# Causal masks of the state-space decays: from mask products on TensorE to ScalarE copies into a PSUM bank of their own

## The chip, the cores and the metric

The kernel runs on one core of one Trainium2 chip. Its engines work side by side and wait for each other by semaphores: TensorE (PE; its weight loads are shown as PEld), VectorE (DVE), ScalarE (ACT), GpSimd (POOL) and SyncE (SP), which issues the DMAs. The metric is the device time of one execution in microseconds (us), here the median of several runs.

## The reference

Two transformer blocks run one after the other on 256 tokens of width 1024. The first has a mixer of sparse and latent attention, cross attention to a memory, and hierarchical experts. The second block joins the result with 256 context tokens and runs two layers: a Mamba-2 state-space mixer (SSD) over both samples and in both directions, then attention; each followed by an expert layer. The change lies in the SSD, whose core in the reference is this:

```python
a = jnp.moveaxis(dtc * A.reshape(SSD_GROUPS, SSD_HPG), 2, -1)
acum = jnp.cumsum(a, axis=-1)
tri = jnp.tril(jnp.ones((Q, Q), dtype=bool))
seg = jnp.exp(jnp.where(tri, acum[..., :, None] - acum[..., None, :], -jnp.inf))
cb = jnp.einsum('bclgn,bcsgn->bcgls', Cc, Bc)
y_diag = jnp.einsum('bcgrls,bcsgrp->bclgrp', cb[:, :, :, None] * seg, xdt)
```

There are 8 groups of 4 heads, chunks of 128 tokens, a state of 128. The projection ahead of it is 1024 x 6208, with a convolution of width 5 over time and silu; behind it come a gate with silu(z), an RMS norm and an output projection of 2048 x 1024. `seg` is the causal mask and the decay in one: positions after the row's own get exp of minus infinity, which is 0.

## The kernel before, in words

The second block's first layer is the SSD. Features lie on partitions and the 512 tokens (256 context, 256 of the sample) along the free axis. Products whose inputs are float32 are done as three products of split halves (`mm3`, L1301 to L1303), so a projection piece of 128 features is 24 products of 512 columns.

`ssd` first normalises and transposes, then calls `ssd_steps` (L1343), which computes the step sizes dt of all heads (L1301 to L1303 into tile `wdt`), their exp and log chain (L1372 to L1385 on ScalarE and VectorE), the transposes of dt (L1390), the running sums by triangular products (L1401) and, for each of the two directions, the factors of the exponents: `RR` (the rows), `LB` and `FL` (the columns), and the state's coefficients, transposed on TensorE at L1445. Then the eight groups follow. `ssd_project` computes six pieces of 128 features for a group (weight split by ScalarE L1295 and VectorE L1296, convolution, tanh), and `ssd_group` its scan. For a chunk's half and each of its two key blocks `ssd_group` forms three exponents, each as one product of `LBg` and `RR` (L1562): two diagonal ones, forward and backward, and one off the diagonal. On a diagonal exponent the mask (bfloat16, 0 or a large negative number) is added by a second product with the identity into the same bank (L1565). ScalarE takes the Exp (L1567), GpSimd adds both diagonals (L1569), VectorE multiplies with B times C (L1572, tile `M`), and TensorE multiplies M with x into the output (L1575). After the groups `ssd_out` (L1616) projects back.

All order on the engines is set by a scheduler that simulates the program's time line and moves instructions within what their tiles allow; it is not written by hand. So instructions of `ssd_steps`, of group 0's projection, and of neighbouring groups lie mixed in the engines' queues. What limits it are the pools: memory tiles and the eight PSUM banks. All of this layer uses one PSUM pool `four`, with two banks for each of the tags p (projections), y (outputs of a group), b (exponents and small products) and t (transposes and products of the states).

The lines that the change and the prediction touch are L1526 to L1613 in `ssd_group`, L1312 in `ssd`, and the pool in `run`.

Of the kernel before, what the change touches and what calls it, by code (L numbers as in the profile page):

```python
# [22 lines left out]
AF = mybir.ActivationFunctionType  # L23
# [7 lines left out]
T = 256  # L31
# [47 lines left out]
class Net:  # L79
# [1229 lines left out]
    def pool(self, name, side=None):  # L1309
        return self.tc.tile_pool(name=name, bufs=1, side=side, reuse_waits="tile")  # L1310

    def ssd(self, right):  # L1312
        nc, a = self.nc, self.a
        self.piece = -1
        with self.pool("ssdh") as hp, self.pool("ssdx") as xp, self.pool("ssd") as pool, ExitStack() as q:
            tile_, x_ = self.cut(pool), self.cut(xp)
            pp = q.enter_context(self.pool("ssdq", "right"))
            self.ada_tile, self.ada_ps = lambda: self._t(pp, [P, 2 * D], "adaw", 1), "p"
            hT = [self.cut(hp)([P, 8, 512], f"hT{v}", 1, F32R) for v in range(2)]
            for r, xx in ((1, self.ctx_x), (0, self.x)):  # L1320
                rows = self.norm_halves([xx[:, 0], xx[:, 1]], lambda: x_([P, 512], "xbc", 8), self.ctx_r if r else None)
                m, sh = self.mod_cols(0, 0, r)
                self.to_features_mod(rows, m, sh, hT, (1 - r) * T, lambda: x_([P, 512], "z", 4)[:, :T])
            with self.pool("ssdr") as rp:
                self.load_const("const_b", rp)
                tmp_ = self.cut(rp)
                A4 = self.arena(rp, 3)
                self.ada_step(1)
                self.ssd_steps(tile_, tmp_, A4, hT)
            with self.pool("ssdg") as gp:  # L1330
                self.yd = [self.dp.tile([P, 2, 512], F32, name=f"yd{g}") for g in range(7)]
                self.sqa = self.cut(gp)([P, 512], "sqa")
                nc.gpsimd.memset(self.sqa, 0.0)
                for g in range(8):
                    parts = self.ssd_project(g, self.cut(pp), self.cut(xp), hT)
                    if g == 7:
                        q.close()
                        op = right.enter_context(self.pool("ssdo", "right"))
                        self.y7 = self.cut(op)([P, 2, 512], "y7")
                    self.ssd_group(g, *parts, self.cut(gp), self.cut(op) if g == 7 else None)  # L1340
        return self.cut(op), op

    def ssd_steps(self, tile_, tmp_, A4, hT):  # L1343
# [180 lines left out]
    def ssd_group(self, g, xs, BT, CT, zz, tile_, last=None):  # L1524
        nc = self.nc
        dsk, nw = self.colv("ssd_D_2"), self.colv("ssd_norm_w_2")  # L1526
        xtm = tile_([P, 2, 4, P], "xtm", 1)
        for c in range(2):
            p = self.ps("t").rearrange("p (i f) -> p i f", i=4)
            for i in range(4):  # L1530
                nc.tensor.transpose(p[:, i], xs[c][:, i * P:(i + 1) * P], self.ident)
            nc.scalar.activation(xtm[:, c], p, AF.Copy)
        btm = tile_([P, 2, P], "btm", 2)
        p = self.ps("t")[:, :T].rearrange("p (i f) -> p i f", i=2)
        for i in range(2):
            nc.tensor.transpose(p[:, i], BT[:, i * P:(i + 1) * P], self.ident)
        nc.vector.tensor_copy(btm, p)
# [1 line left out]
        for d in range(2):  # L1539
            t = tile_([P, 768], "LBg", 2, F32R)  # L1540
            nc.vector.tensor_scalar(t, self.LB[d], self.grp[:, g:g + 1], None, op0=OP.mult)
            LBg.append(t)
            t = tile_([P, 256], "FLg", 2, F32R)
# [3 lines left out]
        for q in range(2):  # L1547
            p = self.ps("b").rearrange("p (s l) -> p s l", s=2)
            for st in range(2):
                i = 2 * q + st  # L1550
                nc.tensor.matmul(p[:, st], lhsT=BT[:, i * P:(i + 1) * P], rhs=CT[:, q * T:(q + 1) * T],
                                 start=True, stop=True)
            cb = tile_([P, 2, T], "cb", 2)
            nc.scalar.activation(cb, p, AF.Copy, scale=0.25)
            for st in range(2):
                M = tile_([P, 4, T], "M", 2)
                ex = []

                for d, var, lt, diag in ((0, 2 * q + st, st, True), (1, 2 * q + st, st, True),
                                         (st, 4 + q, 1 - st, False)):  # L1560
                    p = self.ps("b").rearrange("p (r l) -> p r l", r=4)
                    nc.tensor.matmul(p, lhsT=LBg[d][:, var * P:(var + 1) * P], rhs=self.RR[d][:, :, 2 * q + lt],  # L1562
                                     start=True, stop=not diag)
                    if diag:
                        nc.tensor.matmul(p, lhsT=self.identb, rhs=self.maskb[:, d], start=False, stop=True)  # L1565
                    e = tile_([P, 4, P], "seg", 3)
                    nc.scalar.activation(e, p, AF.Exp)  # L1567
                    ex.append((e, lt))
                nc.gpsimd.tensor_tensor(ex[0][0], ex[0][0], ex[1][0], op=OP.add)  # L1569
                for e, lt in (ex[0], ex[2]):  # L1570
                    s = slice(lt * P, (lt + 1) * P)
                    nc.vector.tensor_tensor(M[:, :, s], e, cb[:, st, None, s].to_broadcast([P, 4, P]), op=OP.mult)  # L1572
                for c in range(2):
                    for par in range(2):
                        nc.tensor.matmul(yps[c][par * 64:par * 64 + 64, q * T:(q + 1) * T],  # L1575
                                         lhsT=xtm[:, c, 2 * q + st, par * 64:par * 64 + 64], rhs=M[:, 2 * c + par],
                                         start=(st == 0), stop=(st == 1))

        hs = tile_([P, 2, 256], "hs", 1)
        for d in range(2):  # L1580
            p = self.ps("b")[:, :256]
            for i in range(2):
# [5 lines left out]
                                 start=(i == 0), stop=(i == 1))  # L1588
            nc.scalar.activation(hs[:, d], p, AF.Copy)
        for c in range(2):  # L1590
# [2 lines left out]
                nc.tensor.matmul(p[:, d], lhsT=self.pairs[:, c], rhs=FLg[d], start=True, stop=True)  # L1593
            eF = tile_([P, 2, 256], "eF", 2)
            nc.scalar.activation(eF, p, AF.Exp)
            p = self.ps("t").rearrange("p (d l) -> p d l", d=2)
            for d in range(2):
                nc.tensor.matmul(p[:, d], lhsT=hs[:, d, c * P:(c + 1) * P], rhs=CT[:, T:], start=True, stop=True)
            nc.vector.tensor_tensor(eF, eF, p, op=OP.mult)
            y, ch = xs[c], 2 * g + c  # L1600
# [471 lines left out]
    def run(self):  # L2072
# [2 lines left out]
        self.small = "b"  # L2075
        nc = self.nc
        four = dict(p=2, y=2, b=2, t=2)
        with ExitStack() as right, self.psum(**four):
            out_, _ = self.ssd(right)
            ap = self.ctx.enter_context(self.pool("attt"))  # L2080
            with self.pool("ch0") as pool, self.weight_slots(2), ExitStack() as more:
                o = self.choice(0, [(self.ctx_x, 1), (self.x, 0)], pool)
                with self.pool("chs0") as tp:
                    tmp_ = self.cut(tp)
                    self.ssd_out(0, out_)
                    self.choice_route(o, 0, tmp_)
                    self.ssd_out(1, out_)
                    self.attention_tables(ap)
                    right.close()
                    more.enter_context(self.weight_slots(4, "right"))  # L2090
                    self.choice_route(o, 1, tmp_)
                more.enter_context(self.weight_slots(1, "right"))
                self.hold = [self.ctx_x[:, 1, 1023:]] * 2
                with self.pool("chf0") as fp:
                    self.choice_run(o, self.cut(fp))
                self.hold = None
# [56 lines left out]
```

## Time and profile before

| | us |
|---|---|
| median of 3 runs | 2184.37 (2181.54 to 2187.75) |
| the profiled execution | 2188.18 |
| its span | 2186.4 |
| PE busy | 1886.7 (86%) |
| DVE busy | 967.2 (44%) |
| ACT busy | 634.0 (29%) |
| POOL busy | 456.7 (21%) |

The span is the time from the first to the last instruction in the trace; the execution's own time holds 1.8 us more around it. The share of busy time is an average over stages: up to about 1010 us the engines share the work of mixers and the SSD, from 1100 to 1500 and from 1760 to 2100 the expert layers stream weights at 426 GB/s and the DMA engines are busy all the time. The SSD's steps lie at about 464 to 519 us, its groups at 516 to 922, its output projection from 922 on. A matmul's duration in the rows holds its way through the array; in a dense stream the distance between two starts tells what one costs.

### The profile page before, as it was taken

Reading aid. Unit: us, or ns where it says so; the run is one execution under the profiler, and the core shown is the slowest. Engines: PE = TensorE matmul, PEld = TensorE weight load, DVE = VectorE, ACT = ScalarE, POOL = GpSimd, SP = SyncE. Lnnn points to the kernel's source line nnn. Section 1 sums busy time; section 2 is a strip of 40 time slices with the busy share of each in tenths; the row PEclk is TensorE's granted clock in tenths of the full one; section 3 lists DMA queues with packets and bytes.
Section 4 is the critical chain, followed back from the end, with each engine's and each line's share of the span. In section 5 each row is a group of like instructions: output and inputs, shape, how many; then the busy total and the mean of one; then the engine's idle time right before and its main releaser. Section 6 shows DMA issues by size and latency. Waiting matters only on the chain. (4 is left out here: it accounts for less than half of the span.)

```text
span 2186.4 us, 23839 instructions
## 1 busy us (share of the span) xinstructions
PE 1886.7 (86%) x9107; PEld 1033.4 (47%) x9128; DVE 967.2 (44%) x1643; ACT 634.0 (29%) x1174; POOL 456.7 (21%) x483
## 2 busy tenths in 40 slices
PE   7989879989999999889799898997989767667666
PEld 6767644356667777567333333333755411111111
DVE  6776642169777787566322222222676301010101
ACT  6545422154544455444100000001454200000000
POOL 4341020023232333422111111101653100000000
PEclk9999989999999999999899999999899889899989
DMA  7554748853232321275799999997537799999996
GB/s 243 179 191 148 294 171 327 365 166 97 87 107 62 127 92 54 88 237 199 317 428 426 426 427 426 428 427 308 223 126 288 288 428 426 429 427 428 427 425 278
DMA packets 131078, 603.49 MB, mean 276 GB/s; under 512 B 18563, under 2 KB 59222, under 8 KB 92558
## 3 DMA queue, kind: packets, MB, share of 16 engines
q1 hardware_dynamic: 130958, 601.91, 69.7%
q8 instruction: 73, 1.20, 0.2%
q14 instruction: 47, 0.39, 0.0%
HBM read 597.09 MB, written 4.78 MB: 275 GB/s over the span
## 5 line engine op out<-in xcount | busy, mean ns | idle before, releaser
L1818 PE MATMUL ps<-w,xg 128*64 128x512 f32 (+1 forms) x2048 | 452.8, 638 | 111.0 <-DMA w<-in_moe_w_dram 111.0
L1818 PEld LDWEIGHTS ps<-w,xg 128*64 128x64 f32 (+1 forms) x2048 | 130.6, 127 | 394.2 <-issue 236.0
L1871 POOL TENSOR_TENSOR x<-x,o 128x512 f32<-128x512 f32 x24 | 38.9, 1621 | 651.4 <-DVE o L1870 651.4
L1301 PE MATMUL ps<-hT,ws 128*128 128x512 f32 x384 | 157.8, 411 | 3.5 <-DVE ada L1236 3.2
L1302 PE MATMUL ps<-hT,ws 128*128 128x512 f32 x384 | 157.8, 411 | 0.0
L1303 PE MATMUL ps<-hT,ws 128*128 128x512 f32 x384 | 155.9, 406 | 0.0
L1818 PE MATMUL ps<-w,ctx 128*32 128x512 f32 x512 | 107.0, 656 | 36.9 <-DMA w<-in_moe_w_dram 35.9
L1818 PE MATMUL ps<-w,actT 128*64 128x512 f32 x512 | 124.4, 596 | 4.0 <-DMA w<-in_moe_w_dram 2.1
L1861 DVE SCALAR_TENSOR_TENSOR y<-ps,s,y 128x512 fp32r<-128x512 f32 x24 | 17.9, 748 | 247.6 <-ACT y L1860 247.6
L1507 DVE SCALAR_TENSOR_TENSOR conv<-pad,cols,conv 128x512 f32<-128x512 f32 x124 | 111.9, 903 | 2.6 <-ACT conv L1500 0.4
L1860 ACT ACTIVATE y<-ps,s 128x512 fp32r<-128x512 f32 x24 | 16.5, 686 | 322.8 <-PE ps L1818 246.6
L1301 PEld LDWEIGHTS ps<-hT,ws 128*128 128x128 f32 x384 | 73.1, 190 | 25.7 <-issue 4.0
L1870 DVE TENSOR_TENSOR o<-ps,g 128x512 f32<-128x512 f32 x80 | 52.3, 686 | 69.2 <-PE ps L1867 66.2
L1302 PEld LDWEIGHTS ps<-hT,ws 128*128 128x128 f32 x384 | 73.4, 191 | 19.1 <-issue 3.8
L1296 DVE TENSOR_TENSOR ws<-wr,ws 128x1024 fp32r<-128x1024 f32 x48 | 62.3, 1299 | 44.5 <-ACT ws L1295 37.9
L1303 PEld LDWEIGHTS ps<-hT,ws 128*128 128x128 f32 x384 | 73.2, 191 | 18.2 <-issue 1.9
L1818 PEld LDWEIGHTS ps<-w,ctx 128*32 128x32 f32 x512 | 25.2, 115 | 113.4 <-DMA w<-in_moe_w_dram 58.2
L1818 PEld LDWEIGHTS ps<-w,actT 128*64 128x64 f32 x512 | 43.0, 136 | 74.9 <-issue 66.5
L1569 POOL TENSOR_TENSOR seg<-seg,seg 128x512 f32<-128x512 f32 x32 | 47.1, 1471 | 116.5 <-ACT seg L1567 101.7
L1296 DVE TENSOR_TENSOR ws<-w,ws 128x1024 fp32r<-128x1024 f32 x46 | 61.5, 1342 | 22.0 <-ACT ws L1295 21.4
L1567 ACT ACTIVATE seg<-ps 128x512 f32<-128x512 f32 x96 | 54.8, 597 | 51.3 <-PE ps L1562 16.1
L1850 DVE TENSOR_TENSOR ctx<-ctx,ps 128x512 f32<-128x512 f32 x8 | 5.5, 686 | 141.9 <-PE ps L1818 141.9
(639 smaller groups left out, 3712.7 us busy)
## 6 DMA issues: line engine op xcount, KB each, us to landing
w<-in_moe_w_dram SPq DMA_DIRECT2D x164, 2048.0 KB
w<-in_moe_w_dram SPq DMA_DIRECT2D x56, 1024.0 KB
v<-in_ada_w_dram SPq DMA_DIRECT2D x32, 512.0 KB
w<-in_moe_w_up_dram SPq DMA_DIRECT2D x16, 1024.0 KB
w<-in_moe_w_gate_dram SPq DMA_DIRECT2D x16, 1024.0 KB
w<-in_moe_w_down_dram SPq DMA_DIRECT2D x16, 1024.0 KB
wr<-in_ssd_in_w_dram SPq DMA_DIRECT2D x16, 1024.0 KB
w<-in_ssd_out_w_dram SPq DMA_DIRECT2D x32, 512.0 KB
```

The lines of the kernel that those rows point to most:

```text
L1296: (eng or self.nc.vector).tensor_tensor(lo, x, hi.bitcast(F32), op=OP.subtract)
L1301: t.matmul(p, lhsT=L[0], rhs=R[0], start=start, stop=False, **kw)
L1302: t.matmul(p, lhsT=L[0], rhs=R[1], start=False, stop=False, **kw)
L1303: t.matmul(p, lhsT=L[1], rhs=R[0], start=False, stop=stop, **kw)
L1507: nc.vector.scalar_tensor_tensor(seq(cv), pad[:, :, j:j + 256], tap(j), seq(cv), op0=OP.mult, op1=OP.add)
L1567: nc.scalar.activation(e, p, AF.Exp)
L1569: nc.gpsimd.tensor_tensor(ex[0][0], ex[0][0], ex[1][0], op=OP.add)
L1818: nc.tensor.matmul(p[j * S:(j + 1) * S], lhsT=x(k, j), rhs=ws[j // ne][:, j % ne, k % nk, n * 512:(n + 1) * 512], start=(k == 0), stop=(k ...
L1860: nc.scalar.activation(y[:, 0], p, AF.Copy, scale=ws)
L1861: nc.vector.scalar_tensor_tensor(y[:, 1], p, ws, y[:, 0].bitcast(F32), op0=OP.mult, op1=OP.subtract)
L1870: nc.vector.tensor_tensor(o, q, gr[s][:, c], op=OP.mult)
L1871: (nc.gpsimd if i else nc.vector).tensor_tensor(xx[:, i, c], xx[:, i, c], o, op=OP.add)
```

## The change

For the groups alone the PSUM pools are closed and others opened: p and y keep two banks, b has three, and one bank, m, is allotted once as `self.seg` for all diagonal exponents. The tag t is gone in the groups; what used it takes b. After the groups the old four tags are opened again. On a diagonal exponent ScalarE copies the mask into the bank first (L1571 of the new kernel), and the exponents' product (L1572) is added onto it with `start=False`; the mask's own product is gone. The first diagonal of all still has a mask product, once (L1569), so that the bank is marked as written. The Exp (L1575) reads the bank as before.

```diff
@@ -1309,7 +1309,7 @@
     def pool(self, name, side=None):
         return self.tc.tile_pool(name=name, bufs=1, side=side, reuse_waits="tile")
 
-    def ssd(self, right):
+    def ssd(self, right, banks):
         nc, a = self.nc, self.a
         self.piece = -1
         with self.pool("ssdh") as hp, self.pool("ssdx") as xp, self.pool("ssd") as pool, ExitStack() as q:
@@ -1327,6 +1327,10 @@
                 A4 = self.arena(rp, 3)
                 self.ada_step(1)
                 self.ssd_steps(tile_, tmp_, A4, hT)
+            banks.close()
+            banks.enter_context(self.psum(p=2, y=2, b=3, m=1))
+
+            self.seg = self.ps("m").rearrange("p (r l) -> p r l", r=4)
             with self.pool("ssdg") as gp:
                 self.yd = [self.dp.tile([P, 2, 512], F32, name=f"yd{g}") for g in range(7)]
                 self.sqa = self.cut(gp)([P, 512], "sqa")
@@ -1338,6 +1342,8 @@
                         op = right.enter_context(self.pool("ssdo", "right"))
                         self.y7 = self.cut(op)([P, 2, 512], "y7")
                     self.ssd_group(g, *parts, self.cut(gp), self.cut(op) if g == 7 else None)
+            banks.close()
+            banks.enter_context(self.psum(p=2, y=2, b=2, t=2))
         return self.cut(op), op
 
     def ssd_steps(self, tile_, tmp_, A4, hT):
@@ -1526,12 +1532,12 @@
         dsk, nw = self.colv("ssd_D_2"), self.colv("ssd_norm_w_2")
         xtm = tile_([P, 2, 4, P], "xtm", 1)
         for c in range(2):
-            p = self.ps("t").rearrange("p (i f) -> p i f", i=4)
+            p = self.ps("b").rearrange("p (i f) -> p i f", i=4)
             for i in range(4):
                 nc.tensor.transpose(p[:, i], xs[c][:, i * P:(i + 1) * P], self.ident)
             nc.scalar.activation(xtm[:, c], p, AF.Copy)
         btm = tile_([P, 2, P], "btm", 2)
-        p = self.ps("t")[:, :T].rearrange("p (i f) -> p i f", i=2)
+        p = self.ps("b")[:, :T].rearrange("p (i f) -> p i f", i=2)
         for i in range(2):
             nc.tensor.transpose(p[:, i], BT[:, i * P:(i + 1) * P], self.ident)
         nc.vector.tensor_copy(btm, p)
@@ -1558,11 +1564,13 @@
 
                 for d, var, lt, diag in ((0, 2 * q + st, st, True), (1, 2 * q + st, st, True),
                                          (st, 4 + q, 1 - st, False)):
-                    p = self.ps("b").rearrange("p (r l) -> p r l", r=4)
+                    p = self.seg if diag else self.ps("b").rearrange("p (r l) -> p r l", r=4)
+                    if diag and (g, q, st, d) == (0, 0, 0, 0):
+                        nc.tensor.matmul(p, lhsT=self.identb, rhs=self.maskb[:, d], start=True, stop=True)
+                    elif diag:
+                        nc.scalar.activation(p, self.maskb[:, d], AF.Copy)
                     nc.tensor.matmul(p, lhsT=LBg[d][:, var * P:(var + 1) * P], rhs=self.RR[d][:, :, 2 * q + lt],
-                                     start=True, stop=not diag)
-                    if diag:
-                        nc.tensor.matmul(p, lhsT=self.identb, rhs=self.maskb[:, d], start=False, stop=True)
+                                     start=not diag, stop=True, skip_group_check=True)
                     e = tile_([P, 4, P], "seg", 3)
                     nc.scalar.activation(e, p, AF.Exp)
                     ex.append((e, lt))
@@ -1593,7 +1601,7 @@
                 nc.tensor.matmul(p[:, d], lhsT=self.pairs[:, c], rhs=FLg[d], start=True, stop=True)
             eF = tile_([P, 2, 256], "eF", 2)
             nc.scalar.activation(eF, p, AF.Exp)
-            p = self.ps("t").rearrange("p (d l) -> p d l", d=2)
+            p = self.ps("b").rearrange("p (d l) -> p d l", d=2)
             for d in range(2):
                 nc.tensor.matmul(p[:, d], lhsT=hs[:, d, c * P:(c + 1) * P], rhs=CT[:, T:], start=True, stop=True)
             nc.vector.tensor_tensor(eF, eF, p, op=OP.mult)
@@ -2075,8 +2083,9 @@
         self.small = "b"
         nc = self.nc
         four = dict(p=2, y=2, b=2, t=2)
-        with ExitStack() as right, self.psum(**four):
-            out_, _ = self.ssd(right)
+        with ExitStack() as right, ExitStack() as banks:
+            banks.enter_context(self.psum(**four))
+            out_, _ = self.ssd(right, banks)
             ap = self.ctx.enter_context(self.pool("attt"))
             with self.pool("ch0") as pool, self.weight_slots(2), ExitStack() as more:
                 o = self.choice(0, [(self.ctx_x, 1), (self.x, 0)], pool)
```

Behind the diff's places the lines of the new kernel are higher than those of before: L1390 is L1396, L1401 is L1407, L1407 is L1413, L1445 is L1451 (all in the steps), L1562 is L1572, L1567 is L1575, L1575 is L1583, L1587, L1593 and L1598 are L1595, L1601 and L1606, L1606 and L1607 are L1614 and L1615. A mask copy must wait for the Exp before it, and every diagonal product for its copy. The change also moves instructions. Three places on TensorE show how.

The first place is TensorE's queue where the steps begin. `ps_6532` is dt's product, `ps_6652` a product of the modulations, and `ws` are weights of group 0's projection, its first piece going to `ps_6720`. Before:

```order
L1301 MATMUL ps_6532<-hT_1325_6357,wdt_1370_6514 64x512
L1234 MATMUL ps_6652<-adaw_6650,silu_c 32x512 x4
L1301 MATMUL ps_6720<-hT_1325_6357,ws_1425_6716 128x512
L1302 MATMUL ps_6720<-hT_1326_6358,ws_1425_6716 128x512
L1303 MATMUL ps_6720<-hT_1325_6357,ws_1426_6717 128x512
```

In the changed kernel, where group 0's projection goes to `ps_6725`:

```order
L1302 MATMUL ps_6532<-hT_1326_6358,wdt_1370_6514 64x512
L1303 MATMUL ps_6532<-hT_1325_6357,wdt_1371_6515 64x512
L1396 MATMUL ps_6577<-const,w_1383_6561 128x64 x4
L1413 MATMUL ps_6600<-w_1382_6560,rep_6518 128x512
L1407 MATMUL ps_6585<-const_b,a_6576 128x128 x4
L1407 MATMUL ps_6643<-const_b,a_6576 128x128 x4
L1451 MATMUL ps_6628<-const,scol_6625 128x32
L1413 MATMUL ps_6658<-w_1382_6560,rep_6518 128x512
L1451 MATMUL ps_6628<-const,scol_6625 128x32
L1451 MATMUL ps_6686<-const,scol_6683 128x32 x2
L1301 MATMUL ps_6725<-hT_1325_6357,ws_1427_6721 128x512
L1302 MATMUL ps_6725<-hT_1326_6358,ws_1427_6721 128x512
```

All the step products (L1396 to L1451) now stand ahead of the first projection; before, the projection began ahead of dt's last products and its pieces stood between those of the steps, the last L1445 having 144 projection products ahead of it.

The second place is TensorE's queue at the first diagonals of group 6 (`LBg` are its columns, `ps_9911` and `ps_9943` projections of group 7). Before:

```order
L1562 MATMUL ps_9582<-RR_1395_6610,LBg_9556 128x512
L1303 MATMUL ps_9911<-hT_1325_6357,ws_2113_9908 128x512
L1301 MATMUL ps_9911<-hT_1325_6357,ws_2112_9907 128x512
L1302 MATMUL ps_9911<-hT_1326_6358,ws_2112_9907 128x512
L1303 MATMUL ps_9911<-hT_1325_6357,ws_2113_9908 128x512
L1301 MATMUL ps_9943<-hT_1325_6357,ws_2116_9939 128x512
L1562 MATMUL ps_9594<-RR_1395_6610,LBg_9556 128x512
L1565 LDWEIGHTS identb_6524
L1565 MATMUL ps_9594<-maskb_6526,identb_6524 128x512
```

In the changed kernel, where `ps_6706` is the bank of all diagonals, and `ps_9496` to `ps_9509` are the group's transposes:

```order
L1234 MATMUL ps_9839<-adaw_9837,silu_c 32x512 x4
L1537 MATMUL ps_9496<-const,xbc_9289 128x128 x4
L1537 MATMUL ps_9502<-const,xbc_9331 128x128 x4
L1542 MATMUL ps_9509<-const,xbc_9376 128x128 x2
L1572 MATMUL ps_6706<-RR_1395_6610,LBg_9513 128x512
L1242 MATMUL ps_9845<-const,ada_6923 128x128 x4
L1572 MATMUL ps_6706<-RR_1413_6668,LBg_9517 128x512
L1583 MATMUL ps_9105<-M_9177,xtm_9079 64x256 x2
```

Two diagonals of one bank have only the four transposes of L1242 between them; before, five projection products lay between them, and they had two banks.

The third place is TensorE's queue at the end of the groups, where the output projection begins. L1575 (L1583 in the changed kernel) is the product with M, `ws,y` are the output projection's operands. Before, at the end of group 6:

```order
L1562 MATMUL ps_9653<-RR_1413_6668,LBg_9560 128x512
L1587 MATMUL ps_9665<-xw_9666,btm_9551 128x256
L1587 MATMUL ps_9665<-xw_9669,btm_9551 128x256
L1575 MATMUL ps_9564<-M_9620,xtm_9538 64x256 x2
L1575 MATMUL ps_9565<-M_9620,xtm_9538 64x256 x2
L1301 MATMUL ps_10207<-ws_2202_10219,y_2199_10213 128x512
L1301 MATMUL ps_10208<-ws_2202_10219,y_2199_10213 128x512
```

In the changed kernel, at the end of group 7:

```order
L1572 MATMUL ps_6706<-RR_1395_6610,LBg_9943 128x512
L1601 MATMUL ps_10076<-FLg_9945,pairs_6522 128x256
L1601 MATMUL ps_10076<-FLg_9949,pairs_6522 128x256
L1583 MATMUL ps_9951<-M_10003,xtm_9925 64x256 x2
L1583 MATMUL ps_9952<-M_10003,xtm_9925 64x256 x2
L1606 MATMUL ps_10081<-xbc_9834,hs_10043 128x256 x2
L1572 MATMUL ps_6706<-RR_1413_6668,LBg_9947 128x512
L1583 MATMUL ps_9951<-M_10023,xtm_9925 64x256 x2
L1583 MATMUL ps_9952<-M_10023,xtm_9925 64x256 x2
L1301 MATMUL ps_10152<-ws_2141_10164,y_2138_10158 128x512
L1302 MATMUL ps_10152<-ws_2142_10165,y_2138_10158 128x512
L1303 MATMUL ps_10152<-ws_2141_10164,y_2139_10159 128x512
```

Before, the output projection's first products stood behind group 6's last M product and 24 of them ahead of group 7's diagonals; now all stand behind group 7's last M product.

## Rows read from the trace of the kernel before

**Rows 1.** Page, part 1: busy us, share of span, count of each engine.

```profile
PE 1886.7 (86%) x9107; PEld 1033.4 (47%) x9128; DVE 967.2 (44%) x1643; ACT 634.0 (29%) x1174; POOL 456.7 (21%) x483
```

**Rows 2.** Windows: stretch, length, busy (count) of PE, PEld, DVE, ACT, POOL, clock, DMA, GB/s.

```profile
470.00:520.00 50.00, 47.34 (x208) 33.19 (x201) 41.79 (x75) 28.05 (x40) 14.62 (x19) 0.93 0.34 106
516.00:876.00 360.00, 356.32 (x1638) 259.35 (x1657) 277.38 (x342) 180.91 (x297) 109.94 (x142) 1.00 0.28 86
876.00:922.00 46.00, 36.34 (x165) 21.56 (x164) 28.99 (x33) 22.83 (x40) 25.52 (x26) 0.93 0.31 104
1100.00:1500.00 400.00, 369.80 (x1535) 138.22 (x1534) 97.14 (x181) 30.29 (x56) 48.67 (x34) 0.99 1.01 426
```

**Rows 3.** Waits of PE in 516 to 876: us in total, times, longest.

```profile
PE ps L1301 <- DVE ada L1236: 3.2, 1, 3.2
PE ps L1301 <- ACT conv L1500: 0.2, 1, 0.2
```

**Rows 4.** Timeline of PE: start, us, line, tiles; a mask product in the stream.

```profile
867.78 0.40 PE L1562 MATMUL ps<-RR,LBg 128*128 128x512 f32 x1
868.02 0.39 PE L1565 MATMUL ps<-maskb,identb 128*128 128x512 bf16 x1
868.06 0.58 PE L1302 MATMUL ps<-hT,ws 128*128 128x512 f32 x1
868.48 0.39 PE L1303 MATMUL ps<-hT,ws 128*128 128x512 f32 x1
```

**Rows 5.** By source L1565: ns min/median/max, first and last start.

```profile
L1565 PEld LDWEIGHTS <-identb x64: 95/96/149, 526.9 to 913.8; 128*128 128x128 bf16 x64
```

**Rows 6.** Lines in 516 to 922: busy us, mean ns, idle before.

```profile
L1567 ACT ACTIVATE seg<-ps 128x512 f32<-128x512 f32 x96 | 54.8, 597 | 51.3 <-PE ps L1562 16.1 <-PE ps L1565 13.9 <-remote 13.1
...
L1295 ACT ACTIVATE ws<-wr 128x1024 fp32r<-128x1024 f32 x41 | 43.3, 1057 | 49.5 <-PE ps L1302 49.2
```

**Rows 7.** By source L243: ScalarE from memory into PSUM.

```profile
L243 ACT ACTIVATE ps<-x x4: 577/592/602, 2173.6 to 2178.0; 128x512 f32<-128x512 f32 x4
```

**Rows 8.** Timeline of PE in the steps.

```profile
473.00 0.40 PE L1303 MATMUL ps<-hT,wdt 128*64 128x512 f32 x1
...
490.83 0.46 PE L1390 MATMUL ps<-const,w 64*128 64x64 f32 x4
...
501.90 1.94 PE L1234 MATMUL ps<-adaw,silu_c 128*32 128x512 f32 x8 [2.66 <-DMA adaw<-in_ada_w_dram]
...
518.85 0.31 PE L1445 MATMUL ps<-const,scol 32*128 32x32 f32 x2
```

**Rows 9.** Timeline of ScalarE in the steps.

```profile
473.44 0.68 ACT L1372 ACTIVATE w<-ps,cols 64x512 f32<-64x512 f32 x1 [6.13 <-PE ps L1303]
...
498.18 0.59 ACT L1404 ACTIVATE F<-ps 128x512 f32<-128x512 f32 x1
```

**Rows 10.** Timeline of VectorE in the steps.

```profile
498.99 0.35 DVE L1409 COPY s<-F 128x4 f32<-128x4 f32 x1
...
516.17 0.27 DVE L1442 TENSOR_SCALAR scol<-a,s 128x128 f32<-128x128 f32 x1
```

**Rows 11.** Windows: clock after sparse and in denser PE work.

```profile
454.00:460.00 6.00, 2.43 (x9) 1.61 (x9) 5.79 (x15) 3.59 (x9) 5.17 (x7) 0.50 0.95 344
460.00:466.00 6.00, 5.82 (x29) 3.31 (x30) 3.66 (x8) 3.55 (x9) 5.34 (x9) 0.69 0.19 40
```

**Rows 12.** Timeline of PE in the tail of the groups.

```profile
875.27 0.39 PE L1303 MATMUL ps<-hT,ws 128*128 128x512 f32 x1
...
882.01 0.49 PE L1562 MATMUL ps<-RR,LBg 128*128 128x512 f32 x1 [1.44 <-ACT seg L1567]
...
919.09 1.08 PE L1575 MATMUL ps<-M,xtm 128*64 128x256 f32 x8 [0.87 <-DVE M L1572]
...
921.98 0.58 PE L1301 MATMUL ps<-ws,y 128*128 128x512 f32 x1
```

**Rows 13.** Timeline of ScalarE behind the groups.

```profile
932.73 0.72 ACT L1606 ACTIVATE y<-xbc,cols 128x512 f32<-128x512 f32 x1 [2.41 <-DVE xbc L1604]
```

## The prediction

> **What bounds the kernel now.** I read the page's head first: TensorE (PE) is busy 1886.7 us, 86% of the span [rows 1]. Then the windows by stage. The change lies in the state-space layer (SSD), from about 470 to 922 us. From 516 to 876 PE is busy 356.32 of 360 us, while ScalarE (ACT) is busy 180.91 and VectorE (DVE) 277.38 [rows 2]; the waits of PE there are 3.4 us together [rows 3]. So in the groups PE sets the pace, and a product more or less counts in full. From 876 to 922, the tail in which no projection is left as filler, PE is busy 36.34 of 46: chains through ACT set the time there. Before 516, in the step tables, PE is busy 47.34 of 50 only because projections of group 0 are interleaved [rows 2]. Behind the SSD the expert layer is bound by its weight stream (DMA share 1.01 at 426 GB/s [rows 2]), whose slots open as the SSD's memory closes; I therefore carry a shift of the SSD's end over one for one.
>
> **The profiled run and the median.** The profiled execution took 2188.18 us, 1.8 more than its span and 3.8 more than the median 2184.37. All differences below are made on its trace; the result is the median plus their sum. A change under 0.3% (6.6 us) counts as no change, about what a measurement here can tell.
>
> **1. Masks off PE.** Three products and a mask product go by at 867.78, 868.02, 868.06 and 868.48: three starts in 0.70 us, 0.23 us each, the mask product like any other [rows 4]. (Modelled starts differ by pairs; the pitch is the mean.) There are 64 mask products by their weight loads [rows 5]; 63 go. 12 of the diagonals come behind the last projection, where PE waits anyway, so 51 to 52 count: 52 x 0.23 = **-12.0 us**.
>
> **2. Masks onto ACT.** 63 copies of 128x512 into PSUM. No row shows a bf16 source; the nearest write from memory into PSUM took 592 ns, the Exp of the same size out of PSUM 597 [rows 6, 7]. I take 0.59, so 37 us over some 400: ACT goes from about 50% to 59%. Alone, PE's work hides that. Below nothing it cannot go, as ACT is given nothing back.
>
> **3. One bank, one chain.** All diagonals use one bank, so each is copy, product, Exp, copy, product. From one diagonal product to the next lie the Exp 0.60, the copy 0.59 and the product's own 0.50 that must drain: 1.7 us; with one weight split (1.06) queued in between on ACT, 2.75 [rows 6, 7]. Where PE has other products for that long, it does not wait; queued behind a waiting diagonal is all of PE. In the new order five places before the last projection have less. The product times between them add to 1.52, 0.92, 0.69, 1.99 and 0.24 us (the third is the place shown: four 128x128 transposes between). Against 1.7 they lack 3.4 us in all, against 2.75 they lack 8.4. I take **+6**. The lower bound is 0 (the queue drains while the scheduler's other work is late anyway); the upper, every one of 52 late by half a microsecond, 26.
>
> **4. The head loses its filler.** The banks change hands between the steps and group 0, and in the new order all step products stand ahead of the first projection of group 0. Before, 144 projection products (6 pieces of 24, counted in the order) ran beside the steps. Now the steps run alone and the 144 follow. Steps alone: the dt product ends near 471.4, 2 us sooner than 473.4 [rows 8], as the eight projections that stood ahead of its end are gone. The chain from L1372 to the last instruction ahead of the first L1390, 18 links with three table loads of 1.28 on ACT, adds to 12.4 us by its own durations, where before it took 473.44 to 490.83 with convolutions between [rows 8, 9]. Then the transposes, scans and copies to F (the first copy of a sum at 498.18 before [rows 9]), 4.2 us by their own durations; then DVE's part of both directions up to L1442, which took 498.99 to 516.17 before and adds to about 9 without others' work [rows 10]. That puts the last step product at 497, give or take 4, where it was 518.85 [rows 8]. Behind it 144 x 0.231 = 33.3 us and the modulation products 1.6: 531.9 against 519.1, +12.4 to +12.8. The six pieces' convolutions now fall on DVE packed together with group 0's start, a wait of 2.7 like the one PE has there now (2.66 for a DMA at 501.90 [rows 8]): **+15.1**. Bounds: +6 (steps done at 491) to +22 (steps at 501, DVE 6 us late).
>
> After sparse work PE's granted clock was 0.50 in 454-460 and 0.69 in 460-466 [rows 11]: of its two levels, 1.2 and 2.4 GHz, the low one and a mixture. The new head is sparse for 25 us, so its first projections may run slow.
> The Trainium skill (TensorE: Matmul & The Clock Gate, What's actually happening) says that the low level is the default and that sustained activity releases it, which agrees with rows 11; by its rule this head starts its projections low, and the sum would come out about 2 us higher than by the rows' stream pitch.
>
> **5. The tail.** Before, the last projection ends at 875.66 and the last M product at 920.17: 44.5 us, with 24 output-projection products as filler at 884 to 896 (5.5 us) and waits for Exps (1.44 the longest) [rows 12]. In the new order no output product stands ahead of the last M product, group 7's chains start right behind group 6's, and 12 diagonals remain as before. They need 12 x 1.7 = 20.3 us at least; PE's own work there is 36.3 - 5.5 - 2.8 = 28; with the idle of before, 9.7, it would be 37.7. I take 37.0: -7.5. The 24 products come behind it, +5.5. The second pair of split output weights stands on ACT behind the last y scalings (L1614, L1615), which wait for POOL's adds; before, that work came 12 us behind the last M product (L1606 at 932.73, after 2.41 us idle for DVE) under cover of other output products [rows 13]; I take 2 us more (0 to 4). The products left between the last M product and the output projection (920.17 to 921.98 [rows 12]) are gone, -1.9. Together **-1.9** (bounds -8 and +8).
>
> **Sum.** -12.0 + 6 + 15.1 - 1.9 = +7.2: 2186.4 + 7.2 = 2193.6 of span, 2191.6 against the median. I say **2191.5 us**, slightly slower.
>
> **Rivals.**
> A. *The saved slots stay saved.* The steps are done at 493 (head +8.4, no wait behind), no diagonal waits, the tail -3.9: -12.0 + 8.4 - 3.9 = -7.5, 2177. For: ACT is half idle, PE's order leaves more than 1.7 us at all but five places. Against: the steps' chain has few links that can overlap.
> B. *The one bank becomes the bound.* ACT is in order, and a copy behind a weight split or a tanh that itself waits is late again and again: 52 x 0.5 = +26 in place of +6, 2211.5. It decides if the mean distance copy to product exceeds what PE has in between; the mean distance between diagonals is 360/52 = 6.9 us [rows 2], which speaks against.
> C. *The weight stream swallows the shift.* If the expert layer's stream starts at the same time whatever the SSD does, its share of 1.01 [rows 2] hides seven microseconds: 2184 to 2186. Against: the slots of that stream open with the SSD's memory.
>
> The rule on this: the Trainium skill (PSUM — Partial Sum Buffer, PSUM bank collisions raise a hardware error) wants every two engines' accesses to a bank guarded against each other. That is the chain of step 3 as a must; with one bank, by the rule, no overlap at all, which is B if PE lacks other work.
>
> **Chances.** Own forecast 0.54 (its own range 2184 to 2199), A 0.28, B 0.13, C 0.05. Faster by over 0.3% means under 2177.8: 0.17 from A and 0.01 of the own case, 0.18. Slower, over 2190.9: 0.29 of the own case and all of B, 0.42. Between: 0.40. The range goes from 2174 (A with a tail of -7) to 2209 (B with two thirds of its price), leaving out 1 in 10 at each end.
>
> **What would show it.** Masks: no L1565 on PE, ACT rows of 0.59 into ps. Head: last step product near 497, first projection behind it, 24 pieces' products dense until 532, group 0's first exponent some 13 us late. Middle: waits of L1572 on ACT of 3 to 9 us over five or more places; 26 or so means B, under 1 means A. Tail: the last M product 37 us behind the last projection, then dense output products. If the head costs under 8 us or the clock stays at 1.00 through it, step 4 was wrong; if the steps end later than 505, its bound was.

## The result, and the profile after

The changed kernel took 2206.77 us (median; 2205.69 to 2207.46, 4 runs), the kernel before 2183.02 in the same comparison (2181.54 to 2187.75, 4 runs): a ratio of 1.0096, 95% interval 1.0082 to 1.0110. It is slower by some 24 us by the medians (21 by the ratio), where 7 were forecast. The profiled execution has a span of 2204.4 us. Part 1 of its page, which answers to [rows 1]:

```profile
PE 1883.3 (85%) x9065; PEld 1035.2 (47%) x9065; DVE 960.8 (44%) x1643; ACT 665.9 (30%) x1237; POOL 449.6 (20%) x483
```

TensorE is busy 3.4 us less, and ScalarE 31.9 us more.

The windows of the changed kernel, with the columns of [rows 2]: the steps, the first products of group 0, the groups from the sixth piece of group 0 to the last projection, the tail from there to the last M product, and the expert layer.

```profile
470.00:520.00 50.00, 35.32 (x143) 26.04 (x143) 34.93 (x67) 23.42 (x36) 2.95 (x9) 0.77 0.07 22
492.00:500.00 8.00, 7.92 (x27) 6.37 (x28) 5.50 (x13) 1.00 (x4) 0.85 (x1) 0.73 0.00 0
539.00:898.00 359.00, 344.01 (x1580) 255.48 (x1579) 267.02 (x325) 201.04 (x340) 103.42 (x138) 0.98 0.27 83
898.00:940.00 42.00, 30.54 (x131) 16.74 (x129) 26.77 (x34) 27.11 (x50) 24.44 (x26) 0.88 0.44 141
1100.00:1500.00 400.00, 370.88 (x1536) 139.18 (x1537) 99.52 (x191) 30.46 (x57) 48.74 (x34) 0.99 1.01 427
```

PE is idle 15 us of the groups (344.01 of 359), where its waits were 3.4 before [rows 3]. The expert layer is as before. A table of stages says where the time went. The cuts are: the start of dt's first product, the start of the z activation that ends group 0's sixth piece, the end of the last projection, the end of the last M product, the start of the router's first product.

| us | head | groups | tail | output projection | sum |
|---|---|---|---|---|---|
| before | 55.5 | 356.0 | 44.5 | 57.2 | 513.2 |
| changed | 79.8 | 358.9 | 42.2 | 54.8 | 535.7 |
| difference | +24.3 | +2.9 | -2.3 | -2.4 | +22.5 |

Each row is read from one profiled execution. The sum, +22.5, is near the medians' difference of 23.8. The spans differ by 18.0 only, because dt's first product starts at 459.20 in the trace of the changed kernel and at 464.14 in that of before, with the instructions of every engine up to there in the same order. Why it starts earlier is not known; in the traces of all twelve kernels it lies between 458.3 and 464.7. So the stages are compared from that product on.

*Head.* TensorE's timeline of the changed kernel, as in [rows 8]: the last dt product, the first transposes, the last step product and the first projections.

```profile
466.14 0.40 PE L1303 MATMUL ps<-hT,wdt 128*64 128x512 f32 x1
475.77 0.66 PE L1396 MATMUL ps<-const,w 64*128 64x64 f32 x4 [9.24 <-DVE w L1391]
...
492.08 0.39 PE L1451 MATMUL ps<-const,scol 32*128 32x32 f32 x2 [6.25 <-DVE scol L1448]
492.40 0.80 PE L1301 MATMUL ps<-hT,ws 128*128 128x512 f32 x1
492.99 0.63 PE L1302 MATMUL ps<-hT,ws 128*128 128x512 f32 x1
493.42 0.63 PE L1303 MATMUL ps<-hT,ws 128*128 128x512 f32 x1
...
495.98 0.57 PE L1303 MATMUL ps<-hT,ws 128*128 128x512 f32 x1
496.38 0.39 PE L1301 MATMUL ps<-hT,ws 128*128 128x512 f32 x1
496.62 0.39 PE L1302 MATMUL ps<-hT,ws 128*128 128x512 f32 x1
...
499.88 0.39 PE L1301 MATMUL ps<-hT,ws 128*128 128x512 f32 x1
```

The steps run alone, as the order said, and take 25.9 us from the end of dt to the last step product (25.6 were reckoned, 471.4 to 497). Then the first nine projections start at distances of about 0.43 us, half the pace, and those from 496.38 on at 0.23. The clock is 0.73 in that window (above), a mixture of 1.2 and 2.4 GHz, after 26 us of sparse work. The Trainium skill (TensorE: Matmul & The Clock Gate, What's actually happening) has this as its rule, the low clock as the default that activity releases; the trace agrees: the 25th product starts 7.5 us behind the first, where the stream's pace gives 5.5.

*Groups.* The waits of PE between 539 and 898 (us in total, times, longest):

```profile
PE ps L1583 <- DVE M L1580: 9.9, 3, 6.3
PE ps L1301 <- ACT conv L1506: 3.2, 2, 2.4
PE ps L1242 <- DVE ada L1236: 1.2, 1, 1.2
PE ps L1572 <- ACT seg L1575: 0.3, 1, 0.3
```

Two thirds of them, 9.9 us, stand at the M product, which waits for VectorE, and none at an exponent that waits for its copy. By source, the copy and who waited for it in the whole trace (total us, times); PE's 1.7 us lie outside these groups, at 521.83 and 920.99:

```profile
L1571 ACT ACTIVATE ps<-maskb x63: 581/608/632, 508.7 to 933.1; 128x512 f32<-128x512 bf16 x63
...
who waited for it (us, times):
  PEld ps L1572: 4.5, 8
  PE ps L1572: 1.7, 2
```

The longest wait shows what happens. First PE, then VectorE:

```profile
785.20 1.51 PE L1572 MATMUL ps<-RR,LBg 128*128 128x512 f32 x3
792.98 1.54 PE L1583 MATMUL ps<-M,xtm 128*64 128x256 f32 x6 [6.27 <-DVE M L1580]
```

```profile
787.85 1.73 DVE L1612 TENSOR_TENSOR xbc<-xbc,z 128x512 f32<-128x512 f32 x1 [0.62 <-POOL xbc L1611]
789.50 1.75 DVE L1516 SCALAR_TENSOR_TENSOR xbc<-xbc,conv 128x512 f32<-128x512 f32 x1
791.17 1.75 DVE L1580 TENSOR_TENSOR M<-seg,cb 128x512 f32<-128x512 f32 x1
```

Three exponents go off together at 785.20, and the M product, next in PE's queue, has nothing between it and them. The Exp of the last diagonal starts at 787.32 and GpSimd's sum of the two diagonals (L1577) ends at 789.03. But M stands on VectorE behind the gating of the group before (L1612, which waits for GpSimd) and a convolution's end (L1516), each at 1.7 us, so it starts only at 791.17, and PE stands for 6.27 us in all.

*Tail.* The end of the last projection, the last M product, the first output product, as in [rows 12]:

```profile
897.51 0.39 PE L1303 MATMUL ps<-hT,ws 128*128 128x512 f32 x1
...
938.09 1.98 PE L1583 MATMUL ps<-M,xtm 128*64 128x256 f32 x8 [3.24 <-DVE M L1580]
940.00 0.80 PE L1301 MATMUL ps<-ws,y 128*128 128x512 f32 x1
940.59 0.63 PE L1302 MATMUL ps<-ws,y 128*128 128x512 f32 x1
941.02 0.63 PE L1303 MATMUL ps<-ws,y 128*128 128x512 f32 x1
```

42.2 us where 37.0 were forecast, with a wait of 3.24 for M again, and the output products at half the pace behind it.

### The profile page after: what moved, and what is told of

The parts are those of the page before. It is cut to its first block, busy times and chain, and to the rows that moved or that the text cites. A ratio compares the mean times of both kernels' runs of the same rounds, so it can differ in the third digit from the quotient of the medians.

```text
span 2204.4 us, 23786 instructions
## 1 busy us (share of the span) xinstructions
PE 1883.3 (85%) x9065; PEld 1035.2 (47%) x9065; DVE 960.8 (44%) x1643; ACT 665.9 (30%) x1237; POOL 449.6 (20%) x483
## 5 line engine op out<-in xcount | busy, mean ns | idle before, releaser
L1513 DVE SCALAR_TENSOR_TENSOR conv<-pad,cols,conv 128x512 f32<-128x512 f32 x124 | 103.7, 836 | 2.9 <-ACT conv L1506 0.8
L1580 DVE TENSOR_TENSOR M<-seg,cb 128x512 f32<-128x512 f32 x64 | 63.6, 1009 | 29.6 <-ACT seg L1575 27.0
L1295 ACT ACTIVATE ws<-wr 128x1024 fp32r<-128x1024 f32 x48 | 50.8, 1057 | 80.2 <-PE ps L1302 78.0
L1296 DVE TENSOR_TENSOR ws<-w,ws 128x1024 fp32r<-128x1024 f32 x46 | 60.8, 1329 | 25.4 <-ACT ws L1295 25.2
L1577 POOL TENSOR_TENSOR seg<-seg,seg 128x512 f32<-128x512 f32 x32 | 45.4, 1418 | 116.2 <-ACT seg L1575 116.2
```

The lines of the kernel that those rows point to most:

```text
L1295: self.nc.scalar.activation(hi, x, AF.Copy)
L1296: (eng or self.nc.vector).tensor_tensor(lo, x, hi.bitcast(F32), op=OP.subtract)
L1513: nc.vector.scalar_tensor_tensor(seq(cv), pad[:, :, j:j + 256], tap(j), seq(cv), op0=OP.mult, op1=OP.add)
```

## The experiments

Two theories at first. Theory 1: the hand-over of the PSUM banks costs the time, by the head's lost overlap, and the copies are near to free. Theory 2: the chain of copy, product and Exp on the one bank costs it. All ratios are to the kernel before, in the same comparison; intervals are 95%. The edits are shortened to the lines that matter; `...` stands for code that is left out.

**1. Masks as products again, pools as changed** (`masks_back`).

```diff
-elif diag:
-    nc.scalar.activation(p, self.maskb[:, d], AF.Copy)
 nc.tensor.matmul(p, lhsT=LBg[...], rhs=self.RR[...], ...)
+if diag:
+    nc.tensor.matmul(p, lhsT=self.identb, rhs=self.maskb[:, d], start=False, stop=True)
```

> The changed kernel with its PSUM pools, but the mask again added by a product with the identity on TensorE (63 more products, 63 fewer ScalarE copies). Theory 1, the hand-over of the PSUM banks costs the time and the copies are near to free: the step products still stand ahead of all of group 0's projection, so the 19 us of the head stay, and 52 products of 0.23 come back: 2207 + 12 = 2219 us if the 15 us of stalls in the middle belong to the pools. Theory 2, the chain of copy, product and Exp on one bank makes the stalls in the middle (15 us): 2207 + 12 - 15 = 2204 us, with under 5 us of waits on VectorE's M in the groups.

Measured: 2190.60 us, ratio 1.0028 (1.0018 to 1.0039). With 63 more products it is some 15 us faster than the changed kernel (the ratios differ by 0.0068). The head is as long (80.2), but PE does not wait in the groups at all (first line; the second is the tail):

```profile
539.00:893.00 354.00, 354.00 (x1680) 259.82 (x1679) 264.96 (x339) 179.63 (x299) 106.98 (x146) 1.00 0.28 88
893.00:919.00 26.00, 20.54 (x94) 11.43 (x93) 16.15 (x21) 15.88 (x29) 14.96 (x19) 0.93 0.45 144
```

The tail is 25.4 us in place of 42.2. It waits less, and it holds less work: 12 exponents stand behind the last projection, 16 in the changed kernel, and PE is busy 20.5 us there in place of 30.5. The waits go as theory 2 said, but the time fell by more than it forecast (2204); theory 1's "near to free" (2219) is wrong. One bank for all diagonals does no harm by itself.

**2. Group pool from the start, no hand-over at the head** (`no_head_switch`).

```diff
 # in ssd, after ssd_steps
-banks.close()
-banks.enter_context(self.psum(p=2, y=2, b=3, m=1))
-self.seg = ...
 # in run
-banks.enter_context(self.psum(**four))
+banks.enter_context(self.psum(p=2, y=2, b=3, m=1))
+self.seg = ...
 # in ps
+tag = tag if tag in self.pb else "b"
```

> The changed kernel with its group pool (p 2, y 2, b 3, m 1) opened from the beginning of the layer, the steps' t tiles taken from b, so that no bank changes hands between the steps and group 0; copies, one bank and the hand-over at the end stay. Theory 1 (hand-over at the head): projections stand among the steps again, the first piece is ready near 480 and not 501, and the time falls by 15 to 20 us, to 2187 to 2192. Theory 2 (one bank and ScalarE): the head's gain is lost again in the groups' stalls and the time stays above 2200.

Measured: 2195.16 us, ratio 1.0043 (1.0030 to 1.0056). The head is 54.2 us, 25.6 shorter than in the changed kernel, and the last step product is again among the projections (the second fence is the groups' window):

```profile
516.42 0.31 PE L1448 MATMUL ps<-const,scol 32*128 32x32 f32 x2
```

```profile
517.00:875.00 358.00, 344.18 (x1578) 255.77 (x1577) 267.52 (x331) 199.49 (x336) 100.76 (x139) 0.98 0.27 82
```

But in the groups PE still loses 14 us (344.18 of 358 busy), 10.8 of them in three waits for M, as in the changed kernel, and the tail grows to 51.9. So it is shown that the hand-over makes the head long, and that the copies' loss does not come from it. But of the 25.6 us only 11.6 arrive in the median (2206.77 to 2195.16): the tail takes 9.7 of them back. The time fell between the two forecasts, as each theory holds for its part.

**3. No hand-over at the end either** (`no_switch`): as 2, without the second `banks.close()` and its pool.

> As the kernel with the group pool from the beginning, but that pool also stays open to the end of the first expert layer (t tiles from b), so that no bank changes hands at the end of the groups either. Theory 1 with a tail that gains from filler (output products beside group 7): 3 to 5 us under the other kernel without the head's hand-over, about 2184. Rival, the tail is better without filler, as the traces have it now (4.7 us less from the last projection to the next stage): 5 us above it, about 2194. Theory 2: above 2200 as well.

Measured: 2199.11 us, ratio 1.0067 (1.0055 to 1.0080). The rival holds, though the time is 5 us above the 2194 that it gave: the tail is 56.3 us with 24 output products in it as filler, and the time 4 us above experiment 2.

**4. The kernel before with a hand-over at the head alone** (`before_head_switch`).

```diff
 self.ssd_steps(tile_, tmp_, A4, hT)
+banks.close()
+banks.enter_context(self.psum(p=2, y=2, b=2, t=2))
```

> The kernel before with nothing changed but that its PSUM pool (p 2, y 2, b 2, t 2) is closed and opened again between the steps and group 0. Masks are products, all stays in its tags. Theory 1: the head alone costs 19 us, so 2183 + 19 = 2202. Theory 2: hand-over costs little, as the lost overlap is caught up in the groups: 2183 to 2190.

Measured: 2213.73 us, ratio 1.0131 (1.0116 to 1.0146). The head is 79.3, +23.8 as in the changed kernel. But the whole is 12 us above theory 1's 2202. The groups are longer by 17.8 and the tail shorter by 12.8, so the order moved there too. In these groups PE waits for exponents held up by ScalarE, which is no wait on M:

```profile
PE ps L1564 <- ACT cb L1556: 7.2, 6, 1.2
PE ps L1564 <- ACT seg L1569: 4.2, 6, 0.7
```

Here there are neither copies nor one bank, so a new order alone can make waits of 11 us; why it fell so is left open.

**5. Masks as products and no hand-over at the head** (`masks_back_no_head`): the edits of 1 and 2 together.

> Group pool (p 2, y 2, b 3, m 1) from the beginning of the layer, so no hand-over at the head, and masks as products. If the head (19.4 us in the kernel with masks as products and hand-over, by the first group's sixth piece) and the shorter middle and tail of that kernel (21 us under the kernel before, from there to the last M product) add up: 2190.6 - 19 to 22 = 2169 to 2172 us, under the kernel before. Rival, the short tail comes from the late head (the same work of group 0 done in the pause): the gain of the head is lost in the tail, 2183 to 2190.

Measured: 2168.24 us, ratio 0.9918 (0.9903 to 0.9933), faster than the kernel before. Head 53.6, groups 358.9, tail 25.6: in this pair the two effects add up, and the tail is 18.9 us shorter than before with masks as products in both. The tail of this kernel in a window, to be held against the 876 to 922 of [rows 2]:

```profile
876.00:902.00 26.00, 20.01 (x91) 11.64 (x92) 15.74 (x21) 16.09 (x29) 14.36 (x18) 0.93 0.43 144
```

PE has 20 us of work there in place of 36: by the order, 12 exponents stand behind the last projection where before had 18, and no output product. So the new allotment of the banks (exponents of the diagonals in a bank of their own, the rest in three), together with the hand-over at the end of the groups, is a gain of some 16 us, which I had not seen. No run parts the two with masks as products.

Now the question was which part of the copies costs: theory A, ScalarE's added load; theory B, the link from Exp to copy to product on one bank.

**6. ScalarE's load without the link** (`dummy_copies`): experiment 1 and, ahead of each diagonal Exp, `nc.scalar.activation(e, self.maskb[:, d], AF.Copy)` into the Exp's own output tile.

> The kernel with the changed pools and masks as products, plus the 63 mask copies on ScalarE, written into the Exp's own output tile ahead of the Exp, which overwrites them: ScalarE's load of the change without the link from copy to product. Theory A, ScalarE's added load in its fixed order makes the M products late: most of the 16 us between 2190.6 and the changed kernel's 2206.8, plus the 12 us of products, come back: 2205 to 2218. Theory B, only the link Exp, copy, product on the one bank does: 2190 to 2194, PE's waits in the middle under 4 us.

Measured: 2195.21 us, ratio 1.0046 (1.0031 to 1.0061): 0.0018 or some 4 us above experiment 1, with 0.2 us of waits of PE in the groups. These copies are no lighter than those into the bank (median 632 ns, against 608). Theory A is ruled out as the main cause; the 4 us lie in groups longer by 3.5 (357.7) without waits, and, with intervals that overlap, are not settled.

**7. No masks at all** (`no_masks`): the copies are left out of the changed kernel.

```diff
-elif diag:
-    nc.scalar.activation(p, self.maskb[:, d], AF.Copy)
-nc.tensor.matmul(p, ..., start=not diag, ...)
+nc.tensor.matmul(p, ..., start=not (diag and (g, q, st, d) == (0, 0, 0, 0)), ...)
-nc.scalar.activation(e, p, AF.Exp)
+nc.scalar.activation(e, p, AF.Exp, scale=0.0 if diag else 1.0)
```

> The changed kernel without the 63 copies; the causal masks are left out and the diagonal exponents are taken with scale 0, so that all stays finite. One bank, the hand-over and the Exps stay. If the copies (by load or by link) are what costs in the middle and tail: as the kernel with masks as products less 63 products, 2190.6 - 12 to 15 = 2176 to 2179. If one bank for all diagonals costs by itself: waits on M of over 8 us stay in the middle and the time is 2190 or more.

Measured: 2178.96 us, ratio 0.9971 (0.9962 to 0.9981). No wait on M is left in the groups. Groups and tail are 364.8 us against 379.6 in experiment 1: 14.8 us for 63 products, 0.235 each, the pitch of [rows 4].

**8. Two mask banks** (`two_banks`): the changed kernel with one bank for each direction.

```diff
-banks.enter_context(self.psum(p=2, y=2, b=3, m=1))
-self.seg = self.ps("m").rearrange("p (r l) -> p r l", r=4)
+banks.enter_context(self.psum(p=2, y=2, b=2, m=2))
+self.segs = [self.ps("m").rearrange("p (r l) -> p r l", r=4) for _ in range(2)]
-p = self.seg if diag else self.ps("b").rearrange("p (r l) -> p r l", r=4)
+p = self.segs[d] if diag else self.ps("b").rearrange("p (r l) -> p r l", r=4)
-if diag and (g, q, st, d) == (0, 0, 0, 0):
+if diag and (g, q, st) == (0, 0, 0):
```

The first diagonal of each bank keeps its mask product, so there are 62 copies.

> The changed kernel with two mask banks, one for the forward and one for the backward diagonals, and two b banks in place of three. Theory B (the link on one bank): forward and backward run side by side, the waits on M in the middle fall from 10 to under 4 us: 2190 to 2198. Theory A (ScalarE's load): unchanged, 2204 to 2210; above that, the third b bank was worth something.

Measured: 2180.75 us, ratio 0.9983 (0.9973 to 0.9992), some 25 us under the changed kernel (0.0113 by the ratios), about twice what theory B gave. The copies are there, and PE does not wait in the groups:

```profile
546.00:892.00 346.00, 346.00 (x1618) 256.56 (x1617) 266.85 (x338) 208.49 (x355) 104.45 (x144) 1.00 0.28 87
```

347.2 us for the groups and 23.8 for the tail, where one bank had 358.9 and 42.2. The head is as long as ever (81.4). Theory B is shown, with its effect on the tail added. The third b bank, which this kernel gives up, does not explain it: with masks as products, two b banks are 12 us slower than three (experiments 10 and 5, both without the hand-over at the head).

**9. Two mask banks and no hand-over at the head** (`two_banks_no_head`): the edits of 2 and 8.

> The copies of the change, one bank for forward and one for backward diagonals, and the group pool (p 2, y 2, b 2, m 2) from the beginning of the layer, so no hand-over at the head. If the two causes are separate, 2180.8 - 19 to 22 = 2159 to 2162 us. Rival: with two b banks for the steps' transposes too, part of the head's gain is lost, 2165 to 2172.

Measured: 2168.27 us, ratio 0.9924 (0.9907 to 0.9940). It beats the kernel before, and equals experiment 5. The gain is 12.5 where 19 to 22 were expected: the head is 61.1 in place of 54, which was the rival (that two b banks leave the steps less room is argued, not shown). What lies behind the router's first product is 1214.8 us long where before had 1209.0 and two banks with the hand-over 1211.9; that is not explained.

**10. The same with masks as products** (`two_banks_products`).

> The same pools and start, with the masks as products: what the copies are worth where neither the link nor the head costs. By 52 to 63 products of 0.23 us this is 12 to 15 us above the kernel with copies. Rival: the copies take as much from ScalarE as they give to TensorE, and both are within 4 us.

Measured: 2180.35 us, ratio 0.9978 (0.9966 to 0.9989): 12.1 above experiment 9. So with these pools, where neither one bank's link nor the hand-over at the head costs, the copies give what 52 products of 0.23 us are worth. But the fastest kernel with products (experiment 5, 2168.24) has the time of the fastest with copies (experiment 9, 2168.27): what the copies take off TensorE, the bank that they need gives away again.

## Why the prediction was right or wrong

The direction was right and the size was not: +7.2 were reckoned by stages, +22.5 measured by stages. By the stages' sums of the experiments (513.2 before; 497.0 in 5; 517.6 in 1; 535.7 changed) the way from before to changed is: -16.2 for the new allotment of the banks with the hand-over at the end, +20.6 for the hand-over at the head, +18.1 for copies in place of products; and the last is -14.6 for the products (503.0 in 7, against 1) and +32.7 for the copies. These prices depend on the way that is taken. Over experiment 2 (521.4) the copies come to +24.4 and the hand-over to +14.3, and in the kernel before the hand-over alone is +28.8 (542.0 in 4).

The stated range, 2174 to 2209, holds 2206.77, but the range of the own forecast, 2184 to 2199, does not. The upper end stood for rival B, and B's way of costing was not what the rows show: that part is luck.

- *Step 1, masks off PE, -12.0.* Right: 12.1 by experiments 9 and 10, and 14.8 in groups and tail for all 63 by experiment 7 against 1.
- *Step 2, copies on ScalarE, 0.59 each and hidden.* The duration is right (median 608 ns). Alone, as a load, they cost some 4 us (nothing to 8 by the two intervals, experiments 6 and 1).
- *Step 3, one bank, one chain, +6.* The step that failed. In size: 15 us of waits in the groups, and experiment 8 gives back 11.7 in the groups and 18.4 in the tail. In place: I looked for exponents that wait for their copy, in five places before the last projection. PE has none there between 539 and 898; in the whole trace such waits are 1.7 us, at two places, and those of the weight loads ahead of exponents 4.5 us, at eight. The waits are mostly (9.9 us) those of M products behind VectorE's queue. The three kernels with copies into one bank (changed, 2 and 3) all have three such waits, of 9.9 to 10.8 us together. They go away with the second bank. That the scheduler built such an order because it saw the chain is argued only; that the one bank with copies is the cause is shown by experiments 1, 6, 7 and 8, each with no such wait in the groups. Of the tail's share the waits are the smaller part: its order leaves 10 us more of PE's work behind the last projection (experiment 1).
- *Step 4, the head, +15.1.* Mechanism right, mis-sized: +24.3. The steps alone took what was reckoned, 25.9 us for 25.6, though by two errors that cancel: the chain up to the first transposes took 9.2 where 12.4 were reckoned, the rest 16.7 where 13.2 were. The six pieces behind them took 46.5 us (492.4 to 538.9) in place of 34.9: 2.0 for the low clock, 3 for waits, and the rest for products of group 0's scan and of the modulations that stand between. The sentence on the clock, which was kept out of the sum, would have brought 2 of them.
- *Step 5, the tail, -1.9.* -4.7 with the output projection, near in size by luck: the tail lost 2.3 where 7.5 were reckoned, and the output projection lost 2.4 where 5.6 more were reckoned. The allotment with the hand-over at the end took 18.9 off the tail (experiment 5) and the copies put 16.8 back (25.4 in experiment 1, 42.2 here). Neither was in the sum.
- *Rivals.* A had the head too cheap. B named the right place (the one bank) and, with 26, a price nearer to the 32.7 than the forecast's 6. But its mechanism, copies that come late on ScalarE, is not what PE waited for, and its point of decision, the mean distance of diagonals, was the wrong measure: the distance was ample and the order used it badly. C did not come: 1209.0 and 1209.5 us follow the router's first product.

## What to carry to other kernels

Where a scheduler sets the order, an edit is priced by three things apart: the work it takes off, the links it adds to a chain on one buffer, and the barriers that its pools put between stages; here, on one way from before to changed, they were -15, +33 and +21, beside -16 from a new allotment of buffers. The parts do not simply add: the same hand-over cost 14 to 29 us by the kernel it stood in, and copies were dearer than products in one allotment and cheaper in another. So compare the best kernel of each kind; here both came out at 2168. Closing a PSUM pool in the middle of overlapped work was a barrier here: no projection started before the last step product (492.40 behind 492.08). A wait shows at the instruction that stands next in the queue, often not at the one that the new dependency belongs to, so undo the dependency, not the wait, to find its price.

## What was not expected of the hardware

A ScalarE copy of 128x512 from bfloat16 into a PSUM bank takes 608 ns, against 592 for float32 [rows 7]: half the bytes give nothing. And an operation of VectorE of one form takes longer or shorter by its neighbours: `M<-seg,cb` has a mean of 854 ns in the groups of before and 1009 in those of the changed kernel. Those with no GpSimd instruction beside them took 676 to 693 ns in both; those beside one up to 1605 and 1787. This is not what made the changed kernel slower: the mean is 969 in the faster experiment 1 and 755 in the slowest, experiment 4. By lines, of before and of the changed kernel:

```profile
L1572 DVE TENSOR_TENSOR M<-seg,cb 128x512 f32<-128x512 f32 x64 | 53.7, 854 | 31.2 <-ACT seg L1567 20.8 <-POOL seg L1569 10.1
```

```profile
L1580 DVE TENSOR_TENSOR M<-seg,cb 128x512 f32<-128x512 f32 x64 | 63.6, 1009 | 29.6 <-ACT seg L1575 27.0 <-POOL seg L1577 2.6
```
